# A gated two-branch decoder layer on one core: tanh loads ahead of two stores, a temporary in another pool, and two operand splits moved from VectorE's early slot to GpSimd

## The chip, the core and the metric

The kernel runs on one core of a Trainium2 chip. The core has TensorE (PE, matmuls; PEld are its weight loads), VectorE (DVE), ScalarE (ACT), GpSimd (POOL) and SyncE (SP), which here only issues DMAs. Every engine works through its own instructions in the order of the program, and waits on semaphores for the others. The metric is the device time of one execution in microseconds (us). Before the change it is 1189.9 us, the median of three runs (1187.22 to 1190.38).

## The reference

One layer on x of 1024 positions by 1024 features, in float32, with weights for everything:

```
h = rmsnorm(x)
q, k, v, u, s, gate_a, gate_b = split(h @ w_in)
A = sliding-window attention(q, k, v)          # width 512
B = chunked spatial gating(u, s)               # width 512
x = x + (sigmoid(gate_a) * (A @ w_oa) + sigmoid(gate_b) * (B @ w_ob)) @ w_out
x = x + (silu(conv_g) * conv_v) @ w_down,      conv = causal width-3 conv of rmsnorm(x) @ w_up
```

The change lies between the two gates (the last columns of `h @ w_in`) and the two branch products `A @ w_oa` and `B @ w_ob`.

## The kernel before, in words

**Exact float32 by halves.** Every matmul operand is split into a high part (a rounded copy, made by ScalarE: `copy_hi`, L89) and a low part (the operand less its high part, a subtraction on VectorE or GpSimd). A product is then three matmuls, high by high, high by low, low by high, of 128 x 128 by 128 x 512.

**Seven products for eight.** The large products are 2 x 2 block products in the Strassen-Winograd form: seven block products named after their left operands, A11, S3, A12, S1, A22, S2 and S4 (`Blocks.prod`, L1061), with the right operands B11, T3, B21, T1, T4, T2 and B22. T1 to T4 are sums of blocks of the right matrix. A pair of output tiles lives in two PSUM tiles, zg and zv, with halves g0, g1, v0, v1. The sums around the products are:

- x1: a copy of g0 after A11 (ScalarE); x7: a copy of v0 after S3 (ScalarE); both in SBUF
- x7 = x7 - g1 after S1 (VectorE, through the helper at L622); S4 then adds into g1
- v1 = x1 + v1 after S2, u2 = copy of v1 (ScalarE), then v0 - u2 and x7 - v1 (VectorE)
- g1 = u2 + g1 after S4 (`last_sum`, L1080 in gates, L1327 in branch units)

**Gates.** `gate_pair` (L1108) computes one pair of tiles, tile c of gate a and of gate b, for c = 1 to 7; `v_end` does c = 0. A product of a gate is 12 matmuls. Its last operands S2 and S4 come from the tile gax. The results go through ScalarE's tanh into an SBUF tile th and from there to DRAM (`gate_out`, L1090 and L1092: tanh, then a store dth<-th issued by SyncE). The last pair's last sum and its two stores are in `gates_end` (L1247), which runs inside the first branch unit. x7, u2, gax and some low parts of weights live in the pool `gp`, which `gates_close` closes; in its place it opens the pool `mg`, with two tanh tiles t0 and t1 (4 KB per partition each) and one merge tile. gax was the first tile of `gp`, 8 KB per partition.

**Branch units.** Eight units (`B_UNITS`) of two output tiles each: (b,0), (b,1), (a,0), (b,2), ... A unit has two jobs: the first holds A11, S3, A12 and S1, the second A22, S2 and S4. A product is 6 matmuls. So unit 0 is jobs 0 and 1, unit 1 jobs 2 and 3, unit 2, the first of branch a, jobs 4 and 5. After its products a unit multiplies its tiles by 1 + tanh (L1334 for branch b, L1336 for branch a: the merges), with th tiles that `th_load` (L1265) loaded back from DRAM, two for each unit: unit 0's and every other even unit's into t0 and t1, the odd units' into the ring of th tiles.

**The order around the change.** `run_jobs` (L713) writes it out by hand. For job i: the job's matmuls and the ScalarE copies among them; the DMAs of job i + 4 (wj<-wb on SyncE); the split of job i + 2's weights (two pieces: wjh on ScalarE, wjl on GpSimd at L1287); then the rest of the job (the subtraction x7 - g1 in a first job; the last sum and the merges in a second job). Hooks put further work into these places: key (u, "x") of unit u's first job ahead of the subtraction, and ahead of the weights' split; (u, 0) at the end of the first job; (u, 1) at the end of the second job. The hooks split the right operands of branch a (`y_split`, L1230: high part on ScalarE, low part on VectorE or, where named, on GpSimd), which unit 2 is the first to use. In the trace their sources are named ya (B11, B21, B22, T3) and ta (T1, T4, T2).

Of the kernel before, what the change touches and what calls it, by code (L numbers as in the profile page):

```python
# [10 lines left out]
F = mybir.dt.float32  # L11
# [30 lines left out]
def body(ctx, tc, nc, a):  # L42
# [8 lines left out]
    def nm(s):  # L51
        uid[0] += 1
        return f"{s}_{uid[0]}"
# [34 lines left out]
    def copy_hi(dst, src, scale=1.0):  # L88
        return nc.scalar.activation(dst, src, AF.Copy, scale=scale)  # L89
# [137 lines left out]
    for k in range(8):  # L227
        x1 = xr[k]
# [392 lines left out]
    def sub(eng, out, x, y, op=ALU.subtract):  # L621
        eng.tensor_tensor(out, x, y, op=op)  # L622
        return out
# [79 lines left out]
    def job_load(i):  # L703
        if i < len(jobs):
            job_w[i] = jobs[i][0]()

    def job_split(i):
        if i < len(jobs):
            job_w[i] = jobs[i][1](job_w[i])
# [22 lines left out]
    s3_pool = s3_cm.__enter__()  # L732
# [170 lines left out]
    pools = {"dr": dr}  # L903
# [10 lines left out]
    def wb_add(j):  # L914

        br, i = divmod(j, 3)
        e, o = d_wb[br, 0], d_wb[br, 1]
        out, src = ((o, a["wb"][br, 2:4].rearrange("b p m -> (b p) m")), (e[128:256], o[128:256]),
                    (e[0:128], e[128:256]))[i]
        nc.gpsimd.dma_start(out, src, accum_op=ALU.add, max_dma_last_dim=4096)  # L920
# [122 lines left out]
    class Blocks:  # L1043
# [17 lines left out]
                    nc.tensor.matmul(o, p[:, k, :], m, start=not more and k == 0 and j == 0,  # L1061
                                     stop=k == nk - 1 and j == 2, skip_group_check=True)

        def temps(self):
            return (p.tile([128, 512], F, tag=t, name=nm(t))
                    for p, t in ((s3_pool, "x1"), (pools["gp"], "x7"), (pools["gp"], "u2")))

        def sums(self, x1, x7, m4):

# [18 lines left out]
    def gate_out(key, z):  # L1088
        t = pools["ls"].tile([128, 1024], F, tag="th", name=nm("th"), bufs=3)
        nc.scalar.activation(t, z, AF.Tanh, scale=0.5)  # L1090
        d = d_th[key] = pools["dr"].tile([128, 1024], F, tag=f"th{key}", name=nm("dth"))
        nc.sync.dma_start(d, t)  # L1092
# [9 lines left out]
    def gates_close():  # L1102
        pools["gp_cm"].__exit__(None, None, None)
        del pools["AX"]
        pools["mg_cm"] = tc.tile_pool(name="mg", bufs=1)
        pools["mg"] = pools["mg_cm"].__enter__()

    def gate_pair(c, prev):  # L1108
        w = g_left[c]
        nx = g_left[c + 1] if c < 7 else None  # L1110
        q = Blocks(w.w, xb)
        x1, x7, q.u2 = q.temps()
        prev.last_sum()
        q.prod(q.g0, "A11", "B11")
        if nx:
            nx.load_q()
        else:
            job_load(0)
            job_load(1)
        nc.scalar.copy(x1, q.g0)  # L1120
        if c == 1:
            gate_out(("a", 0), prev.zv)
        w.split_r()
        gate_out(("b", c - 1), prev.zg)
        if nx:
            wb_add(c - 1)
        y_sums(c, 0)
        q.prod(q.v0, "S3", "T3")
        nc.scalar.copy(x7, q.v0)
        if not nx:  # L1130
            y_split("b", "B11")
            y_split("b", "T3")
        q.prod(q.g0, "A12", "B21", more=True)
        if nx:
            nx.sums_q()
            nx.split_p()
            nx.split_s3()
        else:
            job_split(0)
            job_load(2)  # L1140
        q.prod(q.g1, "S1", "T1")
        sub(nc.vector, x7, x7, q.g1)
        y_sums(c, 1)
        if nx:
            nx.sums_r()
        else:
            zr_cm[0].__exit__(None, None, None)
            pools["mr_cm"] = tc.tile_pool(name="mr", bufs=1, side="right", reuse_waits="tile")
            pools["mr"] = pools["mr_cm"].__enter__()
            ta_load()  # L1150
            y_split("b", "B21")
            y_split("b", "T1")
        q.prod(q.v0, "A22", "T4", more=True)
        if nx:
            nx.split_q()
        else:
            y_split("a", "B11")
            job_split(1)
        if c == 1:
            ya_load()  # L1160
        if c < 6:
            g_left[c + 2].load_p()
        q.prod(q.v1, "S2", "T2")
        q.sums(x1, x7, q.v0)
        if not nx:
            y_split("b", "T4")
            y_split("b", "T2")
            job_load(3)
        if nx:
            gate_out(("a", c), q.zv)  # L1170
        q.prod(q.g1, "S4", "B22", more=True)
        if not nx:
            y_split("b", "B22")
            job_load(4)
        return q
# [7 lines left out]
    def y_src(br, n):  # L1183
        if (br, n) in y_raw:
            return y_raw[br, n]
        y = uT if br == "b" else yb["raw"]
        return y[:, 2 * (n[1] == "2"):2 * (n[1] == "2") + 2, L if n[2] == "1" else H]
# [23 lines left out]
    def y_sums(c, e):  # L1211
        n = Y_SUMS.get((c, e))
        if n:
            y_sum(n[0], n[1:])

    def ta_load():
        t = pools["mr"].tile([128, 4, 1024], F, tag="mh0", name="ta")
        pools["mr"].tile([128, 96], F, name="pad_m")
        for i, n in enumerate(("T1", "T4", "T2")):
            nc.sync.dma_start(t[:, i, :], d_ta[n])  # L1220
            y_raw["a", n] = t[:, i, :].rearrange("p (a b) -> p a b", a=2)

    def y_split(br, n, eng=nc.vector):
        i, j = Y_PLACE[br + n]
        if i not in y_slot:
            y_slot[i] = (U if i == 6 else Y)(f"y{i}", R, [128, 2, 4, 512])
        t = yb[br][n] = y_slot[i][:, j]
        src = y_src(br, n)
        copy_hi(t[:, 0:2], src)
        eng.tensor_tensor(t[:, 2:4], src, t[:, 0:2].bitcast(F), op=ALU.subtract)  # L1230

    def ya_load():
        yb["raw"] = Y("ya", F)
        for t in range(4):
            nc.sync.dma_start(yb["raw"][:, t, :], d_ya[t])

    def gates():
        q = v_end()
        for c in range(1, 8):
            q = gate_pair(c, q)  # L1240
        un["hooks"][0, "x"] = lambda: gates_end(q)
        un["hooks"][0, 0] = lambda: y_split("a", "B21", nc.gpsimd)
        un["hooks"][1, "x"] = lambda: (y_split("a", "T3"), y_split("a", "T1"))
        un["hooks"][1, 0] = lambda: (y_split("a", "T4"), y_split("a", "T2", nc.gpsimd))
        un["hooks"][2, "x"] = lambda: y_split("a", "B22")

    def gates_end(q):  # L1247
        gate_out(("a", 7), q.zv)
        q.last_sum()
        gate_out(("b", 7), q.zg)  # L1250
        gates_close()
        th_load(0)

    B_UNITS = [("b", 0), ("b", 1), ("a", 0), ("b", 2), ("a", 1), ("b", 3), ("a", 2), ("a", 3)]
    ms = {}
# [1 line left out]
    def th_load(u):  # L1257
        br, j = B_UNITS[u]
        for e in (0, 1):
            if u % 2:  # L1260
                t = pools["ls"].tile([128, 1024], F, tag="th", name=nm("th"), bufs=3)
            else:
                t = pools["mg"].tile([128, 1024], F, tag=f"t{e}", name=nm("th"))
            th[u, e] = t
            nc.sync.dma_start(t, d_th[br, 2 * j + e])  # L1265
# [24 lines left out]
    un = {"late": None, "hooks": {}}  # L1290
# [666 lines left out]
    with tc.manual_schedule():  # L1957
        v_phase()
        psum["H"] = None
        gates()  # L1960
        run_jobs()
        mlp()
# [70 lines left out]
```

## Time and profile before

| what | us |
|---|---|
| median of three runs | 1189.9 |
| the profiled execution, its own time | 1185.87 |
| its span | 1184.2 |
| TensorE busy | 1169.8 |
| VectorE busy | 874.7 |
| GpSimd busy | 630.3 |
| ScalarE busy | 566.4 |

The span runs from the first to the last instruction of the profiled execution; the rest of its time lies outside. The granted TensorE clock was full over the whole span. A line of the timeline reads: start in us from the span's start, duration in us, engine, source line, operation, output tile <- input tiles, shapes, and how many instructions were merged into it; in brackets, idle time of the engine just before it and what ended that. In the table by stretch the columns are the stretch, its length, then for each engine the busy time and the count, the granted clock, the busy share of the DMA engines, and GB/s. An interesting stretch is 380 to 410 us: unit 0 begins at 379.78 and unit 2 ends its products at 410.75.

### The profile page before, as it was taken

Reading aid. Unit: us, or ns where it says so; the run is one execution under the profiler, and the core shown is the slowest. Engines: PE = TensorE matmul, PEld = TensorE weight load, DVE = VectorE, ACT = ScalarE, POOL = GpSimd, SP = SyncE. Lnnn points to the kernel's source line nnn. Section 1 sums busy time; section 2 is a strip of 40 time slices with the busy share of each in tenths; the row PEclk is TensorE's granted clock in tenths of the full one; section 3 lists DMA queues with packets and bytes.
Section 4 is the critical chain, followed back from the end, with each engine's and each line's share of the span. In section 5 each row is a group of like instructions: output and inputs, shape, how many; then the busy total and the mean of one; then the engine's idle time right before and its main releaser. Section 6 shows DMA issues by size and latency. Waiting matters only on the chain.

```text
span 1184.2 us, 15918 instructions
## 1 busy us (share of the span) xinstructions
PE 1169.8 (99%) x5842; PEld 990.8 (84%) x5842; DVE 874.7 (74%) x1037; ACT 566.4 (48%) x878; POOL 630.3 (53%) x434
## 2 busy tenths in 40 slices
PE   8999999999999999999999999999999999999998
PEld 8989989988888778888888888888888888888887
DVE  7798975743536877578788788877888798875674
ACT  8555667644346553335444443444444445425331
POOL 2367685488884754444967677776767541000000
PEclk9999999999999999999999999999999999999999
DMA  7010135257555764454545445454655268966471
GB/s 280 29 55 19 55 134 209 69 170 233 166 160 169 253 200 160 126 185 142 136 132 166 119 152 145 148 137 137 163 136 166 67 218 294 367 225 196 154 233 67
DMA packets 80798, 188.66 MB, mean 159 GB/s; under 512 B 9168, under 2 KB 16592, under 8 KB 80592
## 3 DMA queue, kind: packets, MB, share of 16 engines
q1 hardware_dynamic: 73008, 167.72, 41.5%
q0 software_dynamic: 7456, 15.73, 8.4%
q10 hardware_dynamic: 256, 4.19, 1.1%
q8 instruction: 46, 0.75, 0.3%
q14 instruction: 32, 0.26, 0.1%
HBM read 146.97 MB, written 49.02 MB: 166 GB/s over the span
## 4 chain that ended last, share of the span: by engine, by line
PE 86%; DVE 5%; POOL 1%; DMA 1%; issue 1%; ACT 0%; SPq 0%; POOLq 0%; DVEq 0%; ACTq 0%
PE pz L1061 52%; PE pd L1847 10%; PE pdy L1847 8%; PE px L95 2%; PE px L93 2%; PE px L94 2%; PE pvs L94 1%; PE pvs L93 1%; PE pvs L95 1%; DMA th<-dth 1%; PE pq L93 1%; PE pq L95 1%; PE pq L94 1%; PE pv L519 1%; DVE ya L531 0%
## 5 line engine op out<-in xcount | busy, mean ns | idle before, releaser
L1061 PE MATMUL pz<-T,qh 128*128 128x512 f32 x472 | 145.6, 390 | 0.0
L1061 PE MATMUL pz<-B,ph 128*128 128x512 f32 x352 | 109.4, 392 | 0.0
L1061 PEld LDWEIGHTS pz<-T,qh 128*128 128x128 f32 x472 | 88.4, 188 | 18.6 <-ACT u L886 0.3
L1020 POOL TENSOR_TENSOR pl<-lp,ph 128x1024 fp32r<-128x1024 f32 x30 | 73.2, 2439 | 53.6 <-ACT ph L89 53.6
L1061 PE MATMUL pz<-T,ql 128*128 128x512 f32 x236 | 91.8, 389 | 0.0
L1020 POOL TENSOR_TENSOR ql<-lq,qh 128x1024 fp32r<-128x1024 f32 x30 | 76.7, 2558 | 9.1 <-ACT qh L89 9.1
L1061 PEld LDWEIGHTS pz<-B,ph 128*128 128x128 f32 x352 | 65.2, 188 | 15.4 <-ACT x L1687 2.3
L1077 DVE TENSOR_TENSOR pz<-pz,rstd_b 128x1024 f32<-128x1024 f32 x60 | 73.9, 1232 | 4.6 <-ACT rstd_b L143 2.5
L1061 PE MATMUL pz<-y,wjh 128*128 128x512 f32 x224 | 69.5, 391 | 2.1 <-DVE x L622 1.8
L1061 PE MATMUL pz<-T,s3h 128*128 128x512 f32 x232 | 71.4, 389 | 0.0
L1061 PE MATMUL pz<-B,pl 128*128 128x512 f32 x176 | 68.6, 390 | 0.0
L1847 PE MATMUL pd<-bh,ah 128*128 128x512 f32 x176 | 68.5, 389 | 0.0
L1847 PE MATMUL pd<-bl,ah 128*128 128x512 f32 x176 | 68.5, 389 | 0.0
L1847 PE MATMUL pd<-bh,al 128*128 128x512 f32 x176 | 68.5, 389 | 0.0
L1061 PE MATMUL pz<-T,AX 128*128 128x512 f32 x264 | 63.4, 389 | 0.0
L1061 PE MATMUL pz<-B,AX 128*128 128x512 f32 x264 | 63.4, 389 | 0.0
L1020 POOL TENSOR_TENSOR s3l<-lq,s3h 128x512 fp32r<-128x512 f32 x20 | 25.9, 1297 | 61.0 <-ACT s3h L89 61.0
L1061 PEld LDWEIGHTS pz<-T,AX 128*128 128x128 f32 x264 | 49.5, 188 | 10.3
L1061 PEld LDWEIGHTS pz<-B,AX 128*128 128x128 f32 x264 | 49.6, 188 | 10.3
L622 DVE TENSOR_TENSOR pz<-pz,u 128x512 f32<-128x512 f32 x37 | 25.9, 700 | 42.6 <-ACT u L1071 36.2
L1287 POOL TENSOR_TENSOR wjl<-wj,wjh 128x512 fp32r<-128x512 f32 (+1 forms) x32 | 40.2, 1277 | 31.6 <-ACT wjh L89 27.1
L1542 DVE SCALAR_TENSOR_TENSOR tg<-pz,cp,tg 128x1023 f32<-128x1023 f32 (+1 forms) x44 | 56.2, 1278 | 0.8
(358 smaller groups left out, 3592.8 us busy)
## 6 DMA issues: line engine op xcount, KB each, us to landing
lp<-wup SPq DMA_DIRECT2D x22, 512.0 KB, 3.8
lq<-wup SPq DMA_DIRECT2D x22, 512.0 KB, 4.1
ra<-wdown SPq DMA_DIRECT2D x44, 256.0 KB, 4.5
b<-T SPq DMA_DIRECT2D x44, 256.0 KB, 3.7
lq<-wup POOLq DMA_DIRECT2D x42, 256.0 KB, 5.3
B<-tv SPq DMA_DIRECT2D x33, 256.0 KB, 2.0
T<-tt SPq DMA_DIRECT2D x33, 256.0 KB, 2.1
b<-B SPq DMA_DIRECT2D x33, 256.0 KB, 3.1
```

Source lines behind the costliest of these rows:

```text
L93: nc.tensor.matmul(out, wh, mh, start=first, stop=False, **kw)
L94: nc.tensor.matmul(out, wh, ml, start=False, stop=False, **kw)
L95: nc.tensor.matmul(out, wl, mh, start=False, stop=last, **kw)
L519: nc.tensor.matmul(o, vhl[:, kb, g, :], w, start=i == 0, stop=i == len(ops) - 1)
L622: eng.tensor_tensor(out, x, y, op=op)
L1020: nc.gpsimd.tensor_tensor(l, r, h.bitcast(F), op=ALU.subtract)
L1061: nc.tensor.matmul(o, p[:, k, :], m, start=not more and k == 0 and j == 0, stop=k == nk - 1 and j == 2, skip_group_check=True)
L1077: nc.vector.tensor_tensor(z, z, rstd_b, op=ALU.mult)
L1287: nc.gpsimd.tensor_tensor(l[:, k], r[:, k], h[:, k].bitcast(F), op=ALU.subtract)
L1542: nc.vector.scalar_tensor_tensor(t[:, j:], p[:, 0:1024 - j], cw[:, ci, 2 - j:3 - j], t[:, j:], op0=ALU.mult, op1=ALU.add)
L1847: nc.tensor.matmul(o[d], p[:, k - k0, m], q[:, k - k0, :], start=new and k == 0 and j == 0, stop=k == HK - 1 and j == 2, skip_group_check= ...
```

## The change

Four edits.

1. `gates_end` closes the gates' pool and issues unit 0's two tanh loads first, and only then does the last gate pair's two tanh activations, its last sum and its two stores. On SyncE's queue the two loads move ahead of the two stores. Order on the other engines stays.
2. So that the pool can be closed by then, the last gate's u2 (`temps`, called with the next gate or None) is taken from `s3_pool` under the tag s3h, which the gate's own S3 high weights use too. And the new pool `mg` lets each tile wait for the earlier users of its own bytes alone, not for all of the closed pool's.
3. T1's split leaves hook (1, "x"), ahead of unit 1's subtraction, where T3's stays alone behind unit 1's x7 copy. T1 goes to hook (1, 0), behind T4's, with its low part on GpSimd; there it stands behind the split of job 4's weights.
4. T2's split, on GpSimd already, moves from hook (1, 0) to the new hook (1, 1), behind the split of job 5's weights and unit 1's merges.

```diff
-        def temps(self):
-            return (p.tile([128, 512], F, tag=t, name=nm(t))
-                    for p, t in ((s3_pool, "x1"), (pools["gp"], "x7"), (pools["gp"], "u2")))
+        def temps(self, more=True):
+            gp = pools["gp"]
+            return (p.tile([128, 512], F, tag=t, name=nm(n))
+                    for n, p, t in (("x1", s3_pool, "x1"), ("x7", gp, "x7"),
+                                    ("u2", gp, "u2") if more else ("u2", s3_pool, "s3h")))
...
-        pools["mg_cm"] = tc.tile_pool(name="mg", bufs=1)
+        pools["mg_cm"] = tc.tile_pool(name="mg", bufs=1, reuse_waits="tile")
...
-        x1, x7, q.u2 = q.temps()
+        x1, x7, q.u2 = q.temps(nx)
...
-        un["hooks"][1, "x"] = lambda: (y_split("a", "T3"), y_split("a", "T1"))
-        un["hooks"][1, 0] = lambda: (y_split("a", "T4"), y_split("a", "T2", nc.gpsimd))
+        un["hooks"][1, "x"] = lambda: y_split("a", "T3")
+        un["hooks"][1, 0] = lambda: (y_split("a", "T4"), y_split("a", "T1", nc.gpsimd))
+        un["hooks"][1, 1] = lambda: y_split("a", "T2", nc.gpsimd)
         un["hooks"][2, "x"] = lambda: y_split("a", "B22")
 
     def gates_end(q):
+        gates_close()
+        th_load(0)
         gate_out(("a", 7), q.zv)
         q.last_sum()
         gate_out(("b", 7), q.zg)
-        gates_close()
-        th_load(0)
```

## The prediction

> **What bounds the kernel now.** The first view is the page: engine totals.
>
> ```profile
> span 1184.2 us, 15918 instructions
> PE 1169.8 (99%) x5842; PEld 990.8 (84%) x5842; DVE 874.7 (74%) x1037; ACT 566.4 (48%) x878; POOL 630.3 (53%) x434
> ```
>
> TensorE is busy 1169.8 of 1184.2 us, so an edit that leaves its matmuls alone can win only the gaps between them. The second view is the list of waits from 380 to 470 us, the last gate's tail and the first six branch units (columns: who waited for whom, total, times, longest).
>
> ```profile
> DVE m L1334 <- DMA th<-dth: 0.8, 1, 0.8
> PE pz L1061 <- DVE x L622: 1.8, 1, 1.8
> ACT x L1303 <- DVE pz L1327: 0.7, 1, 0.7
> PE pz L1061 <- ACT x L1301: 0.2, 1, 0.2
> ```
>
> One wait of TensorE matters there: a product waits once for VectorE's subtraction at L622. The third view is TensorE in order of time.
>
> ```profile
> 394.76 0.62 PE L1061 MATMUL pz<-y,wjh 128*128 128x512 f32 x2
> 396.12 0.62 PE L1061 MATMUL pz<-y,wjh 128*128 128x512 f32 x2
> 397.25 0.39 PE L1061 MATMUL pz<-y,wjl 128*128 128x512 f32 x1
> 399.46 0.73 PE L1061 MATMUL pz<-y,wjh 128*128 128x512 f32 x2 [1.82 <-DVE x L622]
> 403.67 0.72 PE L1061 MATMUL pz<-y,wjh 128*128 128x512 f32 x2
> 407.86 0.61 PE L1061 MATMUL pz<-y,wjh 128*128 128x512 f32 x2
> 409.22 0.61 PE L1061 MATMUL pz<-y,wjh 128*128 128x512 f32 x2
> ```
>
> These are the starts of products: of unit 1 A22, S2 and (after S2's last matmul) S4; of unit 2 A12, S2 and S4. A product takes 396.12 - 394.76 = 1.36 us. S4 could have started at 396.12 + 1.36 = 397.48 and started at 399.46: **1.98 us lost**. The first matmul after a wait costs 0.11 us more (0.73 for two against 0.62). S4 adds into g1, which the subtraction x7 - g1 must have read.
>
> What VectorE did instead:
>
> ```profile
> 391.51 0.69 DVE L1327 TENSOR_TENSOR pz<-u,pz 128x512 f32<-128x512 f32 x1
> 393.04 1.22 DVE L1334 SCALAR_TENSOR_TENSOR m<-th,pz 128x1024 f32<-128x1024 f32 x1 [0.83 <-DMA th<-dth]
> 395.35 1.22 DVE L1230 TENSOR_TENSOR y<-ya,y 128x1024 fp32r<-128x1024 f32 x1
> 396.49 2.32 DVE L1230 TENSOR_TENSOR y<-ta,y 128x1024 fp32r<-128x1024 f32 x1
> 398.73 0.67 DVE L622 TENSOR_TENSOR x<-x,pz 128x512 f32<-128x512 f32 x1
> 399.33 1.69 DVE L1230 TENSOR_TENSOR y<-ta,y 128x1024 fp32r<-128x1024 f32 x1
> 400.94 0.68 DVE L1321 TENSOR_TENSOR pz<-x,pz 128x512 f32<-128x512 f32 x1
> 404.40 2.35 DVE L1334 SCALAR_TENSOR_TENSOR m<-th,pz 128x1024 f32<-128x1024 f32 x2
> 406.67 1.22 DVE L1230 TENSOR_TENSOR y<-ya,y 128x1024 fp32r<-128x1024 f32 x1
> ```
>
> It waited 0.83 us for the first tanh tile, did unit 0's two merges (L1334), the low parts of T3 and T1 (L1230), and only then the subtraction; T4's low part follows, then v1 + x1 (L1321), and after unit 1's merges B22's low part at 406.67.
>
> **GpSimd and the two engines together.**
>
> ```profile
> 393.15 2.01 POOL L1287 TENSOR_TENSOR wjl<-wj,wjh 128x512 fp32r<-128x512 f32 x2
> 394.42 0.75 POOL L1287 TENSOR_TENSOR wjl<-wj,wjh 128x256 fp32r<-128x256 f32 x1
> 395.49 2.24 POOL L1287 TENSOR_TENSOR wjl<-wj,wjh 128x512 fp32r<-128x512 f32 x1 [0.33 <-ACT wjh L89]
> 395.49 4.45 POOL L1287 TENSOR_TENSOR wjl<-wj,wjh 128x512 fp32r<-128x512 f32 x2 [0.33 <-ACT wjh L89]
> 390.79 2.41 POOL L1230 TENSOR_TENSOR y<-ya,y 128x1024 fp32r<-128x1024 f32 x1
> 399.90 3.38 POOL L1230 TENSOR_TENSOR y<-ta,y 128x1024 fp32r<-128x1024 f32 x1
> 403.24 2.00 POOL L1287 TENSOR_TENSOR wjl<-wj,wjh 128x512 fp32r<-128x512 f32 x2
> ```
>
> wjl are the low parts of the weights: job 3's in the first two rows, job 4's in the next two, job 5's in the last; the L1230 rows are B21's and T2's. Ends interlock with VectorE's splits. T3's ends at 396.57, job 4's first half at 397.73 (1.16 later), T1's at 398.81 (1.08 later), the second half at 399.94 (1.13), T4's at 401.02 (1.08), T2's on GpSimd at 403.28 (2.26). So they take turns: whichever began first finishes, and the other then needs its own bare time. VectorE's operations with an operand in PSUM do not take part: both merges from 404.40 ran beside job 5's 2.00 us, which is no longer than job 3's 2.01. The Trainium skill has this as an exclusive lock on a shared port pair (SBUF — State Buffer, section "SBUF: two separate sides"): the first holds it for the whole instruction. The other reading, that each just runs slower, would price T4's split at T1's 2.32 us wherever GpSimd is busy; by it the A12 stall worked out below would be 1.29 us and not 0.53. The ends above bear out the lock.
>
> **The change, part by part.**
>
> *Tanh loads ahead.* Two loads move ahead of both stores on SyncE's queue.
>
> ```profile
> 377.95 1.76 SPq L1279 DMA_DIRECT2D wj<-wb  x4
> 384.24 3.79 SPq L1092 DMA_DIRECT2D dth<-th  x2
> 388.12 2.91 SPq L1265 DMA_DIRECT2D th<-dth  x4
> 397.18 0.80 SPq L1265 DMA_DIRECT2D th<-dth  x2
> 377.06 2.88 PE L1061 MATMUL pz<-x,gax 128*128 128x512 f32 x12
> 380.00:385.00 5.00, 5.00 (x24) 4.13 (x23) 4.97 (x6) 3.50 (x5) 0.00 (x0) 1.00 0.19 61
> 390.00:395.00 5.00, 5.00 (x24) 4.13 (x23) 3.96 (x5) 4.23 (x8) 5.00 (x4) 1.00 0.92 335
> ```
>
> SyncE has nothing to issue from 379.71 to 384.24. The loads' buffers lie where gax was, whose last reader ends at 379.94, so they issue at about 380 (four took 2.91 us, so two take under 1.5) and delay no store. DMA engines are 19% busy then (the column before GB/s), 92% at 390 to 395. A load of this size took 4.79 us in the crowd (388.12 to 392.91); even at that the pair lands by 386, and is needed at 392.24. The 0.83 us wait goes. If the buffers are late, the loads fall back to the old place: the third rival.
>
> *u2 elsewhere; reuse by tile.* The copy into u2 for gate 7 now waits until S3's high weights are read; S3 is the gate's second product and the copy follows the sixth, so some 11 us of matmuls lie between (2.88 us for twelve). Unit 0's own u2, in the same slot, waits for L1080, which is issued two products earlier. Both cost nothing; without the cover, the copy would hold ScalarE and SyncE's stores behind it. Without these two parts the loads would have to wait for that sum: they are what makes the first part possible.
>
> *T1 off VectorE, behind the subtraction.* The merges start at 391.51 + 0.73 = 392.24, T3 reaches the port at 392.24 + 2.31 = 394.55. Job 3's 256-wide part holds it until 395.16, so T3 ends at 396.24, and the subtraction at 396.85, 0.6 us before S4 wants it. **Gain 1.98.**
>
> *What is late next: T2's high part on ScalarE.*
>
> ```profile
> 392.72 1.06 ACT L89 ACTIVATE y<-ya 128x1024 fp32r<-128x1024 f32 x1
> 393.68 1.05 ACT L89 ACTIVATE y<-ta 128x1024 fp32r<-128x1024 f32 x1
> 395.84 1.99 ACT L89 ACTIVATE y<-ta 128x1024 fp32r<-128x1024 f32 x2
> 403.04 0.57 ACT L1301 COPY x<-pz 128x512 f32<-128x512 f32 x1
> ```
>
> T2's hook now stands behind job 5's weights, so its ScalarE copy sits in front of unit 2's x1 copy, which A12 waits for. That is 0.96 us (393.68 - 392.72) put into the chain L1321, u2 copy, job 5's weights, x1 copy, A12, which takes 403.67 - 400.94 = 2.73 now and 3.69 then. T4's high part is ready at 396.89. GpSimd has waited out T3 and finishes job 4's first half at 396.24 + 1.16 = 397.40; T4's low part ends 1.08 later, 398.48; L1321 starts at 398.40. A12 starts at 402.09. TensorE would want it at 397.48 + 3 x 1.36 = 401.56: **0.53 lost**.
>
> *T1 and T2 on GpSimd.* Job 4's second half ends at 398.48 + 1.13 = 399.61, T1 (2.41, as B21) at 402.0, wanted by S1 at 403.5: hidden, by 1.5 us. Job 5's weights end at 403.95, T2 at 406.3. S2 starts at 402.09 + 0.11 + 3 x 1.36 = 406.28 and needs the low part at its second matmul, 0.23 later: hidden by 0.2 us only. But VectorE reaches B22's split at 398.40 + 3.46 + 2.27 = 404.13 (distances as from 400.94 to 404.40 and 406.67 now), T2 has held the port since 403.9, and so B22 ends at 406.3 + 1.08 = 407.38, unit 2's subtraction at 407.98 and S4 starts at 408.03 where TensorE wanted 407.64: **0.39 lost**, and 0.11 for the first matmul. Unit 1's merges would come at 401.86, and their loads (issued at 397.18, at 4.79 us there by 402.0) have lost their slack; a little more lateness only moves B22 about inside the time in which T2 holds the port.
>
> **Sum.** S4 of unit 2 starts at 408.03 instead of 409.22: 1.19 - 0.11 = **1.1 us gained** (1.98, less what comes back). Later products depend on TensorE through the same chains and move along. The profiled execution took 1185.87 us in all (span 1184.2 and 1.67 around it): 1184.8. Against the median of the runs, 1189.9: **1188.8 us**.
>
> **Unknown costs, from both sides.** T2 on GpSimd costs the path between nothing (2.41, no collision) and what GpSimd's row gives with one, 3.38. The x1 chain costs between 0.2 (T4's split free of the port at 396.92 + 1.14, so A12 at 401.75) and, if L1321 comes no earlier than before, 400.94 + 3.69 - 403.67 = 0.96 more than now. I take the values in turn-taking order, since five ends fit it. The bounds together: from 2.1 us gained (1.98 and one 0.11) to 1.0 lost.
>
> **The rivals.**
>
> 1. *All of it stays*: no collision at T4 and B22, and T2's copy finds ScalarE free early enough. For it: bare, T4 would end at 398.14 and B22 at 405.35, a gap of 0.2 us at A12 and none at S4. Against it: GpSimd has work for that whole stretch. 2.1 us: 1187.8.
>
> 2. *GpSimd becomes the bound: slower.* The Trainium skill speaks for this side (GPSIMD Engine Reference, section "4.1 Engine selection"): elementwise work belongs on VectorE, GpSimd being about twice as slow; the trace agrees, with 2.41 us against 1.22. In rows: job 4's weights, one split and job 5's weights took 395.49 to 405.24 before. If T1's split meets a collision as T2's did, that stays, and T2's at 3.38 ends at 408.62. S2's second matmul ran at 407.86 + 0.23 = 408.09 before. It loses from the point where T2 ends after 408.09: 0.53 + 0.11 = 0.6 us, 1190.5. Against it: one VectorE split fewer collides.
>
> 3. *The loads do not come earlier*: buffers wait or the loads share the queue's delay. For it: both stores ahead of them cost SyncE until 388.12 now. Against it: gax is read by 379.94. Then merges start at 393.04, T3 ends at 396.57, the subtraction at 397.2, still in time. L1321 starts at 398.73, A12 at 402.42, T2 ends at 406.7, B22 at 407.7, S4 at 408.4: 0.7 gained, 1189.2. T1's move is thus most of the gain.
>
> **How the numbers follow.** Forecast 0.45, rivals 0.20, 0.20 and 0.15. Every case lies within 0.3% (3.6 us, about what a measurement of this kernel tells from no change) of 1189.9, so the runs' own scatter decides: three lie from 1187.22 to 1190.38 and the profiled one lower, so a new median falls below more easily than above. Below 1186.3: a third of rival 1, a fifth of the forecast, a sixth of rival 3, a tenth of rival 2: 0.21. Above 1193.5: 0.08. Within: 0.71. The range takes the lowest run less 2.1, 1185.1, to the highest plus 1.0, 1191.4.
>
> **What would show it.** Right: two th loads issued near 380; no L1334 wait near 392; unit 1's S4 without a wait at 397.5; an x1 wait before unit 2's A12 of about half a microsecond; B22's split on VectorE over 2 us long and a short wait before unit 2's S4. Wrong: T2's split on GpSimd ending behind S2's second matmul, the loads still at 388, or TensorE gaps elsewhere that before lacks.

## The result, and the profile after

| | before | after |
|---|---|---|
| median of 9 runs each, us | 1189.66 | 1186.33 |
| lowest to highest, us | 1186.87 to 1192.88 | 1185.46 to 1187.24 |
| the profiled execution, its own time, us | 1185.87 | 1185.60 |
| its span, us | 1184.2 | 1183.9 |

The ratio after / before is 0.9977, with a 95% interval from 0.9967 to 0.9987: 2.7 us of 1189.7 (1.5 to 3.9). The quotient of the two medians is 0.9972, inside that interval. Two things in the table do not fit each other: the medians are 3.3 us apart, the two profiled executions 0.3. And the runs of before spread over 6.0 us, those of after over 1.8. Most of what follows is about that.

The page of after, engine totals (engine, busy us, share of the span, count):

```profile
span 1183.9 us, 15918 instructions
PE 1170.9 (99%) x5842; PEld 991.5 (84%) x5842; DVE 874.8 (74%) x1036; ACT 566.3 (48%) x878; POOL 631.8 (53%) x435
```

One split has gone from VectorE to GpSimd, the rest is as it was. The list of waits of after from 380 to 470 us:

```profile
PE pz L1061 <- ACT x L1304: 0.5, 2, 0.3
PE pz L1061 <- DVE x L622: 0.3, 1, 0.3
```

The merge's wait for a tanh tile is gone and the wait of 1.8 us for L622 too. A wait of 0.3 us for the x1 copy and one of 0.3 for another L622 stand in their place (the other 0.2 us of L1304 is in before too, there under L1301). The timeline of after, engine by engine (lines below the edits are 2 to 3 higher: L1232 is the splits' low part, L1290 the weights' low part, L1304 the x1 copy, L1337 the merge):

```profile
380.28 0.80 SPq L1268 DMA_DIRECT2D th<-dth  x2
384.55 3.73 SPq L1094 DMA_DIRECT2D dth<-th  x2
...
396.41 0.62 PE L1061 MATMUL pz<-y,wjh 128*128 128x512 f32 x2
397.77 0.62 PE L1061 MATMUL pz<-y,wjh 128*128 128x512 f32 x2
402.32 0.72 PE L1061 MATMUL pz<-y,wjh 128*128 128x512 f32 x2 [0.31 <-ACT x L1304]
406.55 0.63 PE L1061 MATMUL pz<-y,wjh 128*128 128x512 f32 x2
408.38 0.70 PE L1061 MATMUL pz<-y,wjh 128*128 128x512 f32 x2 [0.30 <-DVE x L622]
...
392.49 2.35 DVE L1337 SCALAR_TENSOR_TENSOR m<-th,pz 128x1024 f32<-128x1024 f32 x2
394.76 1.72 DVE L1232 TENSOR_TENSOR y<-ya,y 128x1024 fp32r<-128x1024 f32 x1
396.41 0.68 DVE L622 TENSOR_TENSOR x<-x,pz 128x512 f32<-128x512 f32 x1
397.21 1.52 DVE L1232 TENSOR_TENSOR y<-ta,y 128x1024 fp32r<-128x1024 f32 x1
404.37 3.26 DVE L1232 TENSOR_TENSOR y<-ya,y 128x1024 fp32r<-128x1024 f32 x1
407.56 0.68 DVE L622 TENSOR_TENSOR x<-x,pz 128x512 f32<-128x512 f32 x1
...
399.84 2.40 POOL L1232 TENSOR_TENSOR y<-ta,y 128x1024 fp32r<-128x1024 f32 x1
402.20 2.00 POOL L1290 TENSOR_TENSOR wjl<-wj,wjh 128x512 fp32r<-128x512 f32 x2
404.16 2.40 POOL L1232 TENSOR_TENSOR y<-ta,y 128x1024 fp32r<-128x1024 f32 x1
...
400.74 1.05 ACT L89 ACTIVATE y<-ta 128x1024 fp32r<-128x1024 f32 x1
401.69 0.57 ACT L1304 COPY x<-pz 128x512 f32<-128x512 f32 x1
```

The two tanh loads are issued at 380.28, ahead of the stores. The five TensorE rows are unit 1's S2 and S4 and unit 2's A12, S2 and S4: S4 follows S2 at once (397.77 - 396.41 = 1.36 us, a product's time). T2's copy on ScalarE (400.74) sits in front of the x1 copy, and A12 waits. B22's split on VectorE takes 3.26 us, since T2's on GpSimd holds the port until 404.16 + 2.40 = 406.56, and S4 of unit 2 waits.

Unit 0's first matmul began at 379.78 in the trace of before and at 380.09 in that of after, 0.31 later; earlier stages differ by up to 1.3 us from execution to execution (379.15 to 380.46 over all traces here). So the table below counts from that matmul. Columns are starts of products in us after it, read from TensorE's timeline:

| kernel | unit 1 S4 | unit 2 A12 | unit 2 S4 | unit 3 A11 |
|---|---|---|---|---|
| before, the first profile | 19.68 | 23.89 | 29.45 | 30.81 |
| before, two more profiles (e1, e11) | 20.96, 20.95 | 26.77, 26.78 | 32.21, 32.23 | 33.57, 33.59 |
| after | 17.68 | 22.23 | 28.29 | 29.75 |
| loads alone (e2) | 19.30 | 23.54 | 29.08 | 30.44 |
| hooks alone (e3) | 17.68 | 22.30 | 28.38 | 29.84 |
| loads, merges 0.6 later (e9) | 19.50 | 23.72 | 29.28 | 30.64 |
| loads, merges 1.8 later (e10) | 20.93 | 26.76 | 32.20 | 33.56 |
| after, two stalls taken out (e4, e8) | 17.73, 17.74 | 21.81, 21.82 | 27.81, 27.26 | 29.17, 29.06 |

Against the first profile of before, unit 3 starts 30.81 - 29.75 = 1.06 us earlier. Behind that point after needs 0.48 us more (774.06 us to the end of the span, 773.58 in before), most of it at one place near 1000 us, where two matmuls start 0.52 us apart and not 0.23. With the 0.31 us late start that leaves 0.27 of the 1.06, and that is the difference of the spans. The second row of the table is what the 2.7 us need besides.

### The profile page after: what moved, and what is told of

Same layout as the page of the kernel before. It is cut to its first block, busy times and chain, and to the rows that moved or that the text cites. A ratio compares the mean times of both kernels' runs of the same rounds, so it can differ in the third digit from the quotient of the medians.

```text
span 1183.9 us, 15918 instructions
## 1 busy us (share of the span) xinstructions
PE 1170.9 (99%) x5842; PEld 991.5 (84%) x5842; DVE 874.8 (74%) x1036; ACT 566.3 (48%) x878; POOL 631.8 (53%) x435
## 4 chain that ended last, share of the span: by engine, by line
PE 83%; DVE 6%; issue 3%; DMA 2%; POOL 1%; ACT 1%; SPq 0%; DVEq 0%; POOLq 0%; ACTq 0%
PE pz L1061 50%; PE pdy L1850 8%; PE pd L1850 7%; PE px L95 2%; PE px L94 2%; PE px L93 2%; PE pvs L94 1%; PE pvs L93 1%; PE pvs L95 1%; DMA wj<-wb 1%; PE pq L93 1%; PE pq L95 1%; PE pq L94 1%; PE pv L519 1%; PE pu L95 1%
## 5 line engine op out<-in xcount | busy, mean ns | idle before, releaser
L622 DVE TENSOR_TENSOR pz<-pz,u 128x512 f32<-128x512 f32 x37 | 25.9, 700 | 42.5 <-ACT u L1073 36.2
L89 ACT ACTIVATE ah<-ra 128x1024 fp32r<-128x1024 f32 (+1 forms) x24 | 23.7, 989 | 69.4 <-DMA ra<-wdown 22.1
```

## The experiments

### Before once more, and each half of the change alone

Before is run unchanged (e1). The loads alone (e2) are edits 1 and 2, with the hooks as before; the hooks alone (e3) are edits 3 and 4, with the loads as before (only added lines are shown; those taken out are in the diff of the change):

```diff
@@ e2 @@
+        pools["mg_cm"] = tc.tile_pool(name="mg", bufs=1, reuse_waits="tile")
...
+        x1, x7, q.u2 = q.temps(nx)
...
     def gates_end(q):
+        gates_close()
+        th_load(0)
@@ e3 @@
+        un["hooks"][1, "x"] = lambda: y_split("a", "T3")
+        un["hooks"][1, 0] = lambda: (y_split("a", "T4"), y_split("a", "T1", nc.gpsimd))
+        un["hooks"][1, 1] = lambda: y_split("a", "T2", nc.gpsimd)
```

> The kernel before, unchanged, as its own experiment: a second trace, and the scatter of its runs. Theory: its runs differ by several us because the tanh tiles of unit 0 land at a different time in each execution and VectorE's merges, and behind them unit 1's S4, wait for them. Then this trace shows a total time within 1186 to 1193 us, and whatever it has above the first trace's 1185.87 us is found as a longer wait of L1334 for the tanh load and a longer wait of S4 (2 us in the first trace). Rival: the scatter sits elsewhere (the loads at the start, the later weights), S4's wait stays at 1.8 to 2.2 us, and the difference is found in other gaps of TensorE. The ratio is 1.000 within 0.002 for both.

> Edits 1 and 2 alone: the two tanh loads ahead of the stores; T1 stays on VectorE ahead of the subtraction. By turn-taking at the port T3 ends at 396.2, job 4's first half at 397.4, T1 at 398.5 and the subtraction at 399.1 (on the clock of the first trace of before), so S4 of unit 1 starts at 399.2 instead of 399.46: only 0.3 us gained in the trace. Theory (tanh loads scatter): the runs nevertheless become as narrow as those with the whole change (2 us from lowest to highest) and the median falls by 1.5 to 2.5 us below before, since the part of the gain that no single trace shows is the wait for the loads. Rival (scatter elsewhere): the median is 0 to 0.5 us below before, with before's 4 to 6 us of scatter.

> Edits 3 and 4 alone: T1 behind the subtraction and on GpSimd, T2 behind job 5's weights; the tanh loads stay behind the stores. In a trace with the loads landing as in the first one: merges at 393.0, T3 ends at 396.6, the subtraction at 397.2, S4 of unit 1 without a wait, unit 2's A12 waits 0.8 to 0.9 us for the x1 copy, unit 3 begins 0.7 us earlier than before. Theory (tanh loads scatter): the runs keep a scatter of 3 us or more, and the median falls by 0.5 to 1.5 us. Rival (scatter elsewhere): the median falls by 0.7 us and the scatter is that of before and of the whole change alike.

| | median, us | lowest to highest, runs | ratio to before, 95% |
|---|---|---|---|
| e1, before again | 1190.11 | 1187.20 to 1190.76, 11 | 1.0006 (0.9997 to 1.0016) |
| e2, loads alone | 1186.95 | 1185.89 to 1187.84, 11 | 0.9981 (0.9973 to 0.9990) |
| e3, hooks alone | 1187.06 | 1185.47 to 1190.28, 12 | 0.9983 (0.9973 to 0.9993) |

The profiled execution of e1 took 1190.44 us in all, and its stretch from 393 to 405 us is another one than in the first profile. VectorE, GpSimd and TensorE of e1 in order of time:

```profile
394.14 2.38 DVE L1334 SCALAR_TENSOR_TENSOR m<-th,pz 128x1024 f32<-128x1024 f32 x2 [1.27 <-DMA th<-dth]
396.44 2.11 DVE L1230 TENSOR_TENSOR y<-ya,y 128x1024 fp32r<-128x1024 f32 x1
398.47 2.28 DVE L1230 TENSOR_TENSOR y<-ta,y 128x1024 fp32r<-128x1024 f32 x1
400.67 0.67 DVE L622 TENSOR_TENSOR x<-x,pz 128x512 f32<-128x512 f32 x1
401.27 2.78 DVE L1230 TENSOR_TENSOR y<-ta,y 128x1024 fp32r<-128x1024 f32 x1
403.98 0.68 DVE L1321 TENSOR_TENSOR pz<-x,pz 128x512 f32<-128x512 f32 x1
...
396.17 3.50 POOL L1287 TENSOR_TENSOR wjl<-wj,wjh 128x512 fp32r<-128x512 f32 x2 [0.35 <-ACT wjh L89]
399.63 3.34 POOL L1230 TENSOR_TENSOR y<-ta,y 128x1024 fp32r<-128x1024 f32 x1
...
401.40 1.12 PE L1061 MATMUL pz<-y,wjh 128*128 128x512 f32 x2 [3.08 <-DVE x L622]
```

The tanh tile came 0.44 us later than in the first profile (the merge waited 1.27 us, not 0.83). That put T3's split (396.44) 0.27 us *behind* job 4's first half (396.17) where it had been 0.14 us ahead (395.35 against 395.49). So GpSimd goes first from there on: T3 takes 2.11 us and not 1.22; T1's takes 2.28, about what it took (2.32), but waits for the second half of job 4's weights and not for the first; and T2's on GpSimd, which stood behind T4's in the first profile, now gets the port ahead of it (it ends at 402.97, T4's at 404.05, 1.08 later). T4's split ends 23.61 us after unit 0's start and not 21.24: **0.44 us at the entrance become 2.37 at T4's end**, and 2.88 at A12. That is most of what sets the two executions apart: e1's is 4.6 us longer, and 2.8 of these arise between unit 0 and unit 3, 0.7 ahead of unit 0 and 1.1 behind unit 3. The Trainium skill's rule (SBUF — State Buffer, section "SBUF: two separate sides"), that the first to come holds the port for the whole instruction, agrees with these ends; the trace adds that the order, once turned, stays turned through four splits.

The loads alone gained only 0.35 us at A12 against the quick profile of before, and yet 2.3 us in the ratio, with a spread of 2 us. T3's split and job 4's weights in e2:

```profile
394.79 1.74 DVE L1232 TENSOR_TENSOR y<-ya,y 128x1024 fp32r<-128x1024 f32 x1
...
395.85 4.04 POOL L1289 TENSOR_TENSOR wjl<-wj,wjh 128x512 fp32r<-128x512 f32 x2 [0.42 <-ACT wjh L89]
```

Edits 1 and 2 hold the entrance at the quick side: T3's split is now 1.06 us ahead. The hooks alone put S4 on time with the loads still late (the merge waited 0.50 us), and unit 3 begins 0.97 us earlier than in the first profile of before, but one of their runs took 1190.28 and they spread over 4.8 us: more than was expected of the median, less steady than the loads. Either half alone gives most of what both give together. That fits one slow order which either half mostly avoids, and it isn't yet a proof.

### Is it the order at the port?

If it is, pushing T3's split later under the early loads must cost nothing as long as it stays ahead of job 4's first half, and must bring back the whole slow order once it is behind. Both kernels are e2 with merges repeated on the same data, so that VectorE is 0.6 us (e9) or 1.8 us (e10) later:

```diff
@@ behind the merge of branch b (L1334 of before) @@
+                    if u == 0 and e == 1:
+                        nc.vector.scalar_tensor_tensor(ms[c], t, 1.0, z, op0=ALU.add, op1=ALU.mult)   # e10 alone
+                        nc.vector.scalar_tensor_tensor(ms[c][:, 0:512], t[:, 0:512], 1.0, z[:, 0:512],
+                                                       op0=ALU.add, op1=ALU.mult)                     # e9 and e10
```

Before was profiled once more beside them (e11).

> Edits 1 and 2 alone (the second experiment), with unit 0's second merge computed again for half its columns: T3's split reaches VectorE 0.6 us later, at 15.3 us after unit 0's start. Theory (order at the port): job 3's last weights hold the port until 15.3 anyway and job 4's first half asks for it at 15.7, so T3 still goes first and nothing moves: S4 of unit 1 and A12 of unit 2 start as in the second experiment (19.3 and 23.5 us after unit 0's start) within 0.2 us, and the median stays at 1187 us. Rival (time simply adds up on VectorE): both are 0.6 us later.

> The same with the second merge computed again whole and then for half its columns: T3's split comes 1.8 us later, at 16.4 us, behind job 4's first half. Theory (order at the port): T3 waits for that half, T1 for the second half, T2 on GpSimd for T1, and T4 on VectorE for T2; S4 of unit 1 starts at 20.9 us after unit 0's start, T4's split takes over 2.5 us, A12 of unit 2 starts at 26.3 to 26.8 us, as in the second trace of before, 2.7 to 3.2 us later than in the second experiment, for 1.8 us of work; the median is 1189.5 to 1190.5 us. Rival (time adds up): A12 1.8 us later, median 1188.7.

> The kernel before once more, for one more trace. Theory (order at the port): it falls into one of two kinds, told by whether T3's split starts on VectorE before or after job 4's first half on GpSimd. Before it: T3 takes 1.2 us, T4 about 1.7, A12 of unit 2 at 23.9 us after unit 0's start and a time of 1186 to 1188 us. After it: T3 about 2.1, T4 about 2.8, A12 at 26 to 27 us and 1189 to 1191 us. Rival: durations and times in between, with A12 following the tanh tile's landing one for one.

The timeline of e9, VectorE and GpSimd:

```profile
395.11 1.22 DVE L1232 TENSOR_TENSOR y<-ya,y 128x1024 fp32r<-128x1024 f32 x1
399.08 1.69 DVE L1232 TENSOR_TENSOR y<-ta,y 128x1024 fp32r<-128x1024 f32 x1
...
395.40 4.29 POOL L1289 TENSOR_TENSOR wjl<-wj,wjh 128x512 fp32r<-128x512 f32 x2 [0.37 <-DMA wj<-wb]
```

and of e10, with TensorE's wait before S4:

```profile
396.48 1.42 DVE L1232 TENSOR_TENSOR y<-ya,y 128x1024 fp32r<-128x1024 f32 x1
397.82 2.28 DVE L1232 TENSOR_TENSOR y<-ta,y 128x1024 fp32r<-128x1024 f32 x1
400.62 2.78 DVE L1232 TENSOR_TENSOR y<-ta,y 128x1024 fp32r<-128x1024 f32 x1
...
400.75 1.18 PE L1061 MATMUL pz<-y,wjh 128*128 128x512 f32 x2 [3.09 <-DVE x L622]
...
395.52 3.50 POOL L1289 TENSOR_TENSOR wjl<-wj,wjh 128x512 fp32r<-128x512 f32 x2 [0.37 <-ACT wjh L89]
398.98 3.34 POOL L1232 TENSOR_TENSOR y<-ta,y 128x1024 fp32r<-128x1024 f32 x1
```

In e9 T3's split begins at 395.11, ahead of job 4's weights at 395.40, takes its bare 1.22 us, and A12 moves by 0.18 us (23.54 to 23.72). In e10 it begins at 396.48, behind them; T4's split takes 2.78 us and A12 comes 3.22 us later, for 1.8 us of added work. At the end of T4's split, to which VectorE comes without waiting for a matmul, it is already 2.72 us later (23.58 after unit 0's start, 20.86 in e2; 21.06 in e9). The runs say the same: e9 1186.36 (1185.42 to 1187.86, 8 runs, ratio 0.9978, 0.9967 to 0.9989), like e2; e10 1189.17 (1188.50 to 1191.64, 10 runs, ratio 1.0000, 0.9990 to 1.0009), like before. With the early loads still in place, the turned order alone gives the whole gain back.

The profile of e11 was of the slow kind too (its merge waited 1.15 us, T3's split took 1.92). VectorE of e11:

```profile
393.26 1.22 DVE L1334 SCALAR_TENSOR_TENSOR m<-th,pz 128x1024 f32<-128x1024 f32 x1 [1.15 <-DMA th<-dth]
395.85 1.92 DVE L1230 TENSOR_TENSOR y<-ya,y 128x1024 fp32r<-128x1024 f32 x1
400.50 2.79 DVE L1230 TENSOR_TENSOR y<-ta,y 128x1024 fp32r<-128x1024 f32 x1
...
395.39 3.50 POOL L1287 TENSOR_TENSOR wjl<-wj,wjh 128x512 fp32r<-128x512 f32 x2 [0.34 <-ACT wjh L89]
```

The seven traces with the hooks of before fall into two kinds with nothing between. Where T3's split came ahead of job 4's weights (the first profile, e2 and e9: 14.68 to 15.57 us after unit 0's start), T4's ended at 20.86 to 21.24. Where it came behind them (e1, e10, e11, and e7 of the next section: 15.92 to 16.65), T4's ended at 23.58 to 23.62 in all four, however late T3 was.

Two of the three profiles of the unchanged kernel are slow ones, and e10, whose merges are made late, has the median of before. The first profile, from which the prediction was worked out, was of the quick kind.

### Is it the clock? A theory that fell

Behind the 3.08 us of idle time in e1 the matmuls of S4 run at about half the clock (granted: 0.53). The table by stretch of e1 (stretch, length, busy us and count of PE, PEld, DVE, ACT and POOL, granted clock, DMA share, GB/s):

```profile
398.30:401.40 3.10, 0.02 (x1) 0.00 (x0) 3.10 (x4) 0.21 (x1) 3.10 (x2) 1.00 1.00 295
401.40:405.00 3.60, 3.60 (x9) 2.83 (x10) 3.26 (x2) 0.25 (x1) 1.57 (x1) 0.53 0.71 242
```

Nine matmuls take 3.60 us, 0.40 each, where nine at full clock take 9 x 0.227 = 2.04 (a product's 1.36 us has six). This looked like the dear part of the slow order: 1.6 us. To separate idle time and clock from the port, after was given one (e5) or two (e6) more splits of T3 ahead of unit 1's subtraction, one execution each:

```diff
-        un["hooks"][1, "x"] = lambda: y_split("a", "T3")
+        def t3_more():
+            y_split("a", "T3")
+            t, src = yb["a"]["T3"], y_src("a", "T3")
+            for _ in range(2):                       # range(1) in e5
+                nc.vector.tensor_tensor(t[:, 2:4], src, t[:, 0:2].bitcast(F), op=ALU.subtract)
+        un["hooks"][1, "x"] = t3_more
```

And before was given work for TensorE in that gap: unit 1's S2 is computed a second time over the first (e7), with the same values, which shortens the idle time by a product.

```diff
+            if u == 1:
+                q.prod(q.v1, "S2", "T2")
```

> The whole change, with T3's low part computed once more on VectorE ahead of unit 1's subtraction. By turn-taking job 4's first half goes between the two, so the subtraction ends at about 399.3 on the clock of the trace after (unit 0 at 380.09) and S4 of unit 1 waits 1.5 us. Theory (TensorE's granted clock falls only behind a wait longer than some 2 to 3 us): the granted clock stays 1.00 in the stretch behind S4, matmuls follow each other at 226 ns, and the trace is 1.2 to 1.6 us longer than that after. Rival (the slow matmuls of the second trace of before come from contention or from another part of the program): they may appear here or not, independent of the wait.

> The same with T3's low part computed twice more: the subtraction ends at about 401.5 and S4 of unit 1 waits 3.5 us. Theory: the granted clock falls to about half behind S4 for some 3.5 us, eight to sixteen matmuls start 427 ns apart and not 226, and the trace is 1.5 to 2 us longer than the wait alone explains, about 5 us above that after. Rival: no fall of the clock at this place, 3.5 us above that after.

> The kernel before, with unit 1's product S2 computed twice into the same PSUM half (the second time over the first, same values): six matmuls more, 1.36 us, placed into the stretch in which S4 waits. Theory (part of before's time is the halved clock behind the long wait): the wait shrinks by 1.36 us, to under 2 us in every execution, S4 starts where it did, the clock stays full, and the median falls by 1 to 1.7 us below before although there is more work; nothing is lost in executions with the short wait, since 1.36 is below 1.98. Rival (the clock plays no part): the median is that of before within 0.5 us, or longer by up to 1.4 us.

TensorE in the timeline of e6, and the stretch behind its wait:

```profile
401.67 1.22 PE L1061 MATMUL pz<-y,wjh 128*128 128x512 f32 x2 [3.58 <-DVE x L622]
...
400.00:405.00 5.00, 3.33 (x8) 2.65 (x9) 4.92 (x4) 0.00 (x0) 3.23 (x1) 0.50 0.61 216
```

In e5 S2 began 16.37 us after unit 0's first matmul, so S4 could have started at 16.37 + 1.36 = 17.73; it is 19.27 - 17.73 = 1.54 us late, and the clock stays full; in e6 S4 is 3.75 us late and the clock falls to 0.50. Their spans are 1185.5 and 1188.6 us, 1.6 and 4.7 above after's. So much was as expected. But e7 was not: 1189.23 us (1186.76 to 1191.51, 11 runs), ratio 1.0001 (0.9990 to 1.0012), where 1 to 1.7 us less had been expected. The timeline of e7, TensorE and VectorE:

```profile
400.11 0.74 PE L1061 MATMUL pz<-y,wjh 128*128 128x512 f32 x2 [1.75 <-DVE x L622]
405.42 0.73 PE L1061 MATMUL pz<-y,wjh 128*128 128x512 f32 x2 [0.89 <-ACT x L1301]
...
395.07 2.15 DVE L1230 TENSOR_TENSOR y<-ya,y 128x1024 fp32r<-128x1024 f32 x1
399.97 2.80 DVE L1230 TENSOR_TENSOR y<-ta,y 128x1024 fp32r<-128x1024 f32 x1
```

The clock stays full, and TensorE then waits 0.89 us at A12, for the x1 copy. What A12 waits for is the chain from T4's split (2.80 us here, in the turned order) over L1321, the u2 copy and job 5's weights to that copy. Slow matmuls run beside that chain. In e1 L1321 starts at 403.98, and the chain's 2.73 us would let A12 start at 406.71; it started at 380.44 + 26.77 = 407.21. The clock costs 0.5 us there at most; the port costs the rest. The trace of e7 has the same price: with the clock full, A12 came 26.26 us after unit 0's start, 0.51 earlier than in e1. So small an effect, in some of the executions, does not show in e7's runs; a gain of more than 1.2 us lies outside their interval.

### Taking out the two stalls that the change leaves

e4 is after with two pieces moved: T2's high part ahead of job 5's weights on ScalarE, and B22's low part behind unit 2's subtraction. e8 is e4 with T2's low part on VectorE.

```diff
-        un["hooks"][1, 0] = lambda: (y_split("a", "T4"), y_split("a", "T1", nc.gpsimd))
-        un["hooks"][1, 1] = lambda: y_split("a", "T2", nc.gpsimd)
-        un["hooks"][2, "x"] = lambda: y_split("a", "B22")
+        un["hooks"][1, 0] = lambda: (y_split("a", "T4"), y_split("a", "T1", nc.gpsimd), y_high("a", "T2"))
+        un["hooks"][1, 1] = lambda: y_low("a", "T2", nc.gpsimd)        # nc.vector in e8
+        un["hooks"][2, "x"] = lambda: y_high("a", "B22")
+        un["hooks"][2, 0] = lambda: y_low("a", "B22", nc.vector)
```

> The whole change, and the two new waits taken out: T2's high part goes back to the end of unit 2's predecessor's first job (so that it is not in front of unit 2's x1 copy on ScalarE), and B22's low part goes behind unit 2's subtraction. If turn-taking at the port and T2's place in ScalarE's order are what gave 0.9 us of the gain back, unit 2's A12 starts without a wait, S4 of unit 2 waits at most 0.3 us, unit 3 begins 0.8 to 1.0 us earlier than with the whole change alone against unit 0, and the time is 0.7 to 1.0 us below it (1185.4). If the waits have another cause they stay at 0.5 and 0.5 us, and the time is that of the whole change, 1186.3.

> As the fourth experiment (the whole change less its two new waits), with T2's low part on VectorE behind unit 1's merges instead of on GpSimd. GpSimd was behind there by 0.4 us at S2 of unit 2. VectorE reaches T2's low part at 24.3 us after unit 0's start and needs 1.1, 0.6 us before S2 wants it; B22's low part, behind the subtraction, can still meet job 6's weights at the port, worth 0.4 us at S4. So the trace gains 0 to 0.5 us on the fourth experiment, and the median lies at 1184 to 1184.5 us; if VectorE is the tighter engine, it loses up to 0.5.

The waits of e4 from 380 to 470 us:

```profile
PE pz L1061 <- POOL y L1238: 0.3, 1, 0.3
PE pz L1061 <- ACT x L1311: 0.2, 1, 0.2
```

A12 and the subtraction no longer hold anything up. What is left in e4 is S2's second matmul, which waits for T2's low part from GpSimd: the margin of 0.2 us that the prediction gave it is gone once A12 comes earlier. e8 ends that one and gets B22's split against job 6's weights instead. Unit 3 starts 0.58 us (e4; 0.8 to 1.0 had been expected) and 0.69 us (e8) earlier than in after. In runs: e4 1184.37 us (1184.23 to 1186.62, 6 runs, ratio 0.9967, 0.9954 to 0.9979), e8 1185.17 us (1184.70 to 1185.91, 6 runs, ratio 0.9968, 0.9956 to 0.9980), where 1184 to 1184.5 had been expected. Both medians are lower than after's, but neither ran in one series with after, and the intervals overlap after's, so no gain in the runs is shown. Four runs of e4 lie within 0.2 us of 1184.3 and two near 1186.5; why is open.

## Why the prediction was right, and where its size was off

The change, step by step, did what was forecast. The times forecast were on the clock of before's trace, so 0.31 us is added to them here for the later unit 0:

| step | forecast + 0.31, us | in the trace of after, us |
|---|---|---|
| tanh loads issued | about 380.3 | 380.28 |
| S4 of unit 1, no wait | 397.79 | 397.77 |
| A12 of unit 2 behind T2's copy on ScalarE | 402.40 | 402.32 |
| T1 on GpSimd ends | 402.3 | 402.24 |
| T2 on GpSimd ends | 406.6 | 406.56 |
| B22's split ends, held by T2 | 407.69 | 407.63 |
| S4 of unit 2 | 408.34 | 408.38 |
| unit 3 earlier by | 1.1 | 1.06 |

Turn-taking at the port, the rule by which the splits were priced, held at every end. Of the rivals, *all of it stays* fell: of the 1.98 us, the two stalls forecast took 0.9 back. *GpSimd becomes the bound* fell: T2 met no collision and ended at 406.56, and S2's second matmul did not wait. But it is close by, as e4 showed with its wait for T2. *The loads do not come earlier* fell with the first row of the table. The prediction also named TensorE gaps elsewhere, that before lacks, as a sign of being wrong. The one near 1000 us is such a gap, but it is no work of the change: e1 has it too (0.40 us between starts, 0.52 in after).

**Mis-sized: the last step of the sum**, "Against the median of the runs, 1189.9: 1188.8 us". It took a gain worked out from one execution, the profiled one, off a median of other executions. The profiled one had its own time of 1185.87 us, 1.35 below the lowest of the three runs beside it, and that was put down to scatter. In the main it was another order at the port. Against the kind of execution that was profiled, the change gains 1.06 us, as forecast; against the other kind it gains 33.57 - 29.75 = 3.8 us at unit 3. The profiles of before show both, and the measured 2.7 us (1.5 to 3.9) lies between; that a mixture of the two makes up this figure is argued, not shown. The forecast of 1.1 us lies below that interval. That the median of 1186.33 falls inside the range all the same is luck: the range was carried down to the lowest run less 2.1 for the scatter of the runs, not for a second order.

The hint stood in the rows quoted in the prediction: T3's split came to the port 0.14 us ahead of job 4's weights, and it came when it did because of a wait of 0.83 us on a transfer in a stretch where the DMA engines were 92% busy. That wait was valued at what it cost in this one trace, 0.83 us of VectorE, not at what it decided. Edit 1 was called the lesser part ("T1's move is thus most of the gain"). In the trace that holds (0.97 of the 1.06 us with the hooks alone, 0.37 with the loads alone); in the runs the loads alone give 0.9981, the hooks alone 0.9983.

Not settled: how often before falls into either order (three profiles are too few for a share), and the rest of the scatter. Of the 71 runs of before listed beside the change and the experiments, 55 took longer than 1188.2 us, which is the longest run of e2 (1187.84) and the 0.37 us by which unit 3 starts earlier there; that speaks for the slow order being the more frequent one, but it is no count of it. Edits 1 and 2 were run only together, and so were 3 and 4. Part of the scatter is in the stages ahead of unit 0, part at one place in the up-projection, where a product waits for an x1 copy in some executions. In e2, TensorE's waits from 379 to 700 us:

```profile
PE pz L1061 <- DVE x L622: 1.4, 1, 1.4
PE pz L1061 <- ACT x L1689: 1.1, 1, 1.1
```

The second wait is at 594 us; in the first profile of before and in that of after it does not occur. Taking it out was not tried.

## What to carry to other kernels

Before a gain from one trace is taken off a median, compare the profiled execution's own time with the runs: where it lies outside them, look for a place where a small delay decides an order, and work the sum out for the other order too. Where two engines take turns, what counts is by how much the first one wins, and what sets its arrival: a margin of 0.14 us behind a transfer is worth more to secure than the wait itself seems to cost. And an idle engine's slower clock costs only what the next dependency doesn't hide, so it is priced at the next wait and not by its matmuls.

## What the runs showed of the hardware

- VectorE's splits (two operands in SBUF) and GpSimd's operations take strict turns, in the order of arrival: a 128x1024 split on VectorE took 1.22 us bare, and 1.42 (e10) to 3.28 us (e3) where it had to wait its turn. At the end of the last of these splits, T4's, 0.44 us at the first had become 2.37 (e1); 1.8 us of added work had become 2.7 (e10), 0.6 us 0.2 (e9).
- TensorE's granted clock fell to half (0.40 us a matmul in e1's stretch instead of 0.23) behind idle times of 3.08 us (e1 and e11), 3.09 (e10) and 3.58 (e6), and not behind 1.75 (e7) or 1.82 (before). The Trainium skill (TensorE: Matmul & The Clock Gate, section "Part 1: The HAM clock gate (the "warmup" mystery)") states about 3.4 us of idle time for it, in a window that runs freely. The starts either side of the gap lie 3.47 us apart in e1, but the idle time shown, behind the modelled end of a matmul, is 3.08 us, under the figure of the Trainium skill.
